# Recurrence of an RWKV layer: substitution steps at other points, the second head's copies on ScalarE

## The chip, the cores and the metric

One core of one Trainium2 chip runs the whole program. The metric is the device time of one execution in microseconds (us); three runs of the kernel before took 3350.44, 3358.05 and 3355.8 us, so their median is 3355.8 us.

## The reference

The reference is two blocks, one after the other. The first has an RWKV-7 mixer beside a pooling branch, a layer norm and a mixture of experts; the second is two attention layers (grouped queries, then latent attention). The change touches only the mixer's recurrence over 1024 tokens and 12 heads of size 64, cut here to its core:

```python
def rwkv7_step(state, inp):
    r, decay, k, v, kk, a = inp
    sa = jnp.einsum('bhij,bhj->bhi', state, -kk)
    state = (state * decay[:, :, None, :]
             + sa[..., None] * (kk * a)[:, :, None, :]
             + v[..., None] * k[:, :, None, :])
    out = jnp.einsum('bhij,bhj->bhi', state, r)
    return state, out
...
    _, y = lax.scan(rwkv7_step, state0, (tmaj(r), tmaj(decay), tmaj(k), tmaj(v), tmaj(kk), tmaj(a)))
```

What the kernel must give is `y`, for all tokens and heads. It does not step token by token: it takes chunks of 64 tokens, and inside a chunk the steps become a triangular system of 64 equations, whose inverse is worked out ahead.

## The kernel before, in words

**Units and slots.** `phase_units` does the mixer's projections and its recurrence. A unit is one pair of heads over 512 tokens, that is 8 chunks; there are 12 units (6 pairs, two halves of the sequence). The work of a unit is cut into lanes: `project` (the three projections, 72 groups of TensorE products with tile `pz`), `tokens`, `within`, `hand_over`, `solve`, `masks`, `inverse`, `chain`, `finish` and a few single calls. Each lane is a generator, and `PLAN` gives for each of its pieces a point, counted from the start of the unit's chain. Units follow each other every 24 points (`SLOT`). The loop at the end of `phase_units` goes through the points in order, and at each point through the lanes in the order of `ORDER` (within, lt_load, chain, finish, inverse, tokens, hand_over, masks, start_state, solve, project, thload). The order of the instructions on every engine, and of the DMAs on SP's queue, is the order in which this loop writes them; the points have no time of their own.

**The chain.** `chain` of a unit takes 24 points, three for each chunk. At the first, TensorE makes `ry` (L784; tiles `cA` for the first head, `cB` for the second) and both halves are copied from PSUM to `R`; at the second, TensorE multiplies `R` by the inverse (`T64`, L789) and both halves are copied to `XA` and `XB`; at the third, TensorE makes the addition to the state (L796) and VectorE writes the next state into `XA` and `XB` (L798). All four copies of a chunk go through `copy` and are VectorE instructions of line L775. Points -24 to -1 of a unit are the 24 steps of the chain of the unit ahead, so that point -17 is step 7 of that chain, -11 its step 13 and -8 its step 16, and point -25 is the last step of the chain before that.

**The inverse.** The 64x64 system is inverted from its 16x16 diagonal blocks. `within` makes the system (`M`) and stores it to DRAM (`labd`, L656); `lt_load` fetches the diagonal blocks into tile `LT` with four DMAs (L664). `solve` does the substitution in 15 steps on VectorE, each a product (L711) and a sum (L713) over t x t elements for step t; each step needs the one before. Its end stores the result to DRAM (`tnd`, L715) and fetches it back into block form with eight DMAs (L720, tile `T16`; the profile writes `T`). `inverse` begins with two transposes of `T16` on VectorE (L737) and a product with it on TensorE (L742, `pA<-T,L`), and ends in `T64`, which the first L789 of the unit's chain needs.

**Queues.** SP issues nearly all DMAs of the phase, in the written order, and stays at one that waits. TensorE, VectorE and ScalarE also run in the written order. `finish` stores its result with SP at its points 37 and 39, which are steps 13 and 15 of the next chain.

Of the kernel before, what the change touches and what calls it, by code (L numbers as in the profile page):

```python
# [142 lines left out]
def phase_lowrank(g, xh0, xl0):  # L143

    nc, tc, a = g.nc, g.tc, g.a
    with ExitStack() as c:
# [231 lines left out]
        -54, -53, -51, -49],  # L378
    "thload": [-57],
    "hand_over": [-21, -18, -18, -18, -17],  # L380
    "solve": [-22, -22, -22, -22, -22, -20, -20, -20, -20, -20, -20, -19, -18, -18, -17, -17],
    "masks": [-21, -20, -19, -16, -16],
    "inverse": [-8, -7, -4, -3, -2, -2, 0, 0, 0],
    "start_state": [-12],
    "within": [-35, -35, -35, -34, -33, -33, -32, -30],
    "tokens": [-47, -47, -46, -45, -44, -44, -43, -42, -41, -41, -40, -39, -38, -37, -37, -36, -34, -33, -33, -31,
        -31, -31, -29],
    "lt_load": [-24],
    "chain": [0, 1, 2, 3, 4, 5, 6, 7, 8, 9, 10, 11, 12, 13, 14, 15, 16, 17, 18, 19, 20, 21, 22, 23],
    "finish": [26, 27, 29, 30, 31, 32, 32, 32, 35, 37, 38, 39, 40, 41, 42],  # L390
}
# [13 lines left out]
def phase_units(g, xh, xl):  # L405
    nc, tc, a = g.nc, g.tc, g.a
    with ExitStack() as c:
# [12 lines left out]
        lo, hi = slice(0, 64), slice(64, 128)  # L420
# [345 lines left out]
        def chain(v):  # L766

            u, q = U[v], v % NPAIR
            u.Y = hv.tile([P, HC, 64], F32, name="Y")
            u.st = hv.tile([P, HC, 6], F32, name="st")  # L770
            hd = ((lo, u.GA, u.XA, u.TK[0], "cA"), (hi, u.GB, u.XB, u.TK[1], "cB"))

            def copy(sl, out, src):
                if True:
                    nc.vector.tensor_copy(out, src)  # L775
                else:
                    nc.scalar.activation(out, src, AF.Copy)

            for cc in range(HC):
                yy = pC.tile([P, 64], F32, name="yy")  # L780
                R = hv.tile([P, 64], F32, name="R")
                for sl, G, X, TK, tag in hd:
                    ry = pC.tile([P, 64], F32, name=tag)
                    nc.tensor.matmul(ry[sl], G[:, cc, 0, :], X[:, 0, cc, :])  # L784
                    copy(sl, R[sl], ry[sl])
                yield
                for e, (sl, G, X, TK, tag) in enumerate(hd):
                    us = pC.tile([P, 64], F32, name=tag)
                    nc.tensor.matmul(us[sl], T64[:, cc, e, :], R)  # L789
                    copy(sl, X[sl, 1, cc, :], us[sl])  # L790
                for sl, G, X, TK, tag in hd:
                    nc.tensor.matmul(yy[sl], G[:, cc, 1, :], X[:, 0, cc, :], start=True, stop=False)
                yield
                for sl, G, X, TK, tag in hd:
                    sp = pC.tile([P, 64], F32, name=tag)
                    nc.tensor.matmul(sp[sl], TK[:, cc, :], X[:, 1, cc, :])  # L796
                    dst = X[sl, 0, cc + 1, :] if cc + 1 < HC else Sc[sl, q, :]
                    nc.vector.scalar_tensor_tensor(dst, X[sl, 0, cc, :], f[sl, v, cc:cc + 1], sp[sl], op0=OP.mult, op1=OP.add)  # L798
                for e, (sl, G, X, TK, tag) in enumerate(hd):
                    nc.tensor.matmul(yy[sl], u.H[:, cc, e, :], X[:, 1, cc, :], start=False, stop=True)  # L800
                nc.scalar.activation(u.Y[:, cc, :], yy, AF.Copy)
                if cc:
                    nc.vector.bn_stats(u.st[:, cc - 1, :], u.Y[:, cc - 1, :])
                yield
            nc.vector.bn_stats(u.st[:, HC - 1, :], u.Y[:, HC - 1, :])
# [2341 lines left out]
```

## Time and profile before

| | us |
|---|---|
| median of three runs | 3355.8 |
| profiled execution, its own time | 3354.52 |
| its span | 3352.7 |
| TensorE busy in the span | 2974.5 (89%) |
| VectorE busy | 2149.2 (64%) |
| ScalarE busy | 1537.0 (46%) |
| GpSimd busy | 1623.5 (48%) |

The recurrence's first chain matmul starts at 265.6 us of the span and its last chunk's at 860.6 us. In the stretch from 265 to 863 us TensorE is busy for 520.99 of 598.00 us, VectorE for 451.70, GpSimd for 363.71 and ScalarE for 244.95. A matmul's end is modelled, and matmuls overlap, so a busy TensorE is not one at its peak. A gap in brackets behind an instruction is idle time of its engine before it, with what ended it.

### The profile page before, as it was taken

What the parts mean: (1) busy time and instruction counts of PE and PEld (TensorE: products, weight loads), DVE (VectorE), ACT (ScalarE), POOL (GpSimd) and SP (SyncE); (2) the same over time, 40 slices, a digit from 0 to 9 for tenths busy, and PEclk for the clock granted to TensorE, in tenths of its full rate; (3) what the DMA queues carried; (4) which work ended last, traced back from release to release, by engine and by line L of the source; (5) the groups of instructions that cost most, each with busy time, mean ns of one, the idle gap of its engine ahead of it and who ended that gap; (6) DMA issues with size and microseconds to landing.
All of it is one profiled execution on the core that took longest, in us unless ns stands there. A gap on an engine that the chain in (4) does not pass through costs nothing. (4 is left out here: it accounts for less than half of the span.)

```text
span 3352.7 us, 47462 instructions
## 1 busy us (share of the span) xinstructions
PE 2974.5 (89%) x16804; PEld 2080.9 (62%) x16804; DVE 2149.2 (64%) x3471; ACT 1537.0 (46%) x2828; POOL 1623.5 (48%) x1564
## 2 busy tenths in 40 slices
PE   7878888888869997799988988989898889999998
PEld 4356656655657765699854554557677755555557
DVE  2147787786469977866346676767347247676666
ACT  3334344343439967533134444545345334444452
POOL 0065666665435543553134545567446215454465
PEclk9888999988869999799999999999999999999999
DMA  8835555445769998423221111246134311111136
GB/s 292 282 106 124 143 123 128 110 121 152 236 230 334 324 327 299 163 89 99 74 70 38 50 39 51 68 139 220 51 97 147 120 50 62 46 42 42 41 102 222
DMA packets 394066, 457.16 MB, mean 136 GB/s; under 512 B 123319, under 2 KB 301970, under 8 KB 393698
## 3 DMA queue, kind: packets, MB, share of 16 engines
q1 hardware_dynamic: 380032, 426.15, 40.7%
q0 software_dynamic: 7616, 17.09, 1.5%
q10 hardware_dynamic: 6178, 10.86, 0.8%
q8 instruction: 133, 2.18, 0.3%
q14 instruction: 107, 0.88, 0.1%
HBM read 329.40 MB, written 101.11 MB: 128 GB/s over the span
## 5 line engine op out<-in xcount | busy, mean ns | idle before, releaser
L2117 ACT ACTIVATE p<-st 128x512 f32<-128x512 f32 (+1 forms) x672 | 378.1, 584 | 391.9 <-PE st L2115 318.5
L2036 DVE TENSOR_REDUCE mx<-s 128x1 f32<-128x1280 f32 x256 | 380.4, 1486 | 260.8 <-PE s L2035 260.8
L2127 POOL TENSOR_TENSOR acc<-acc,p 128x512 f32<-128x512 f32 x256 | 379.3, 1482 | 128.0 <-ACT p L2117 114.7
L2135 PE MATMUL o<-p,V 128*64 128x512 f32 (+1 forms) x1344 | 318.3, 595 | 0.0
L2127 DVE TENSOR_TENSOR acc<-acc,p 128x512 f32<-128x512 f32 x256 | 285.6, 1116 | 7.6
L1419 DVE TENSOR_TENSOR wl<-wr,wh 128x1024 fp32r<-128x1024 f32 x156 | 227.4, 1487 | 40.3 <-ACT wh L1418 40.2
L103 PE MATMUL pz<-xh,wh 128*128 128x512 f32 x440 | 223.8, 509 | 7.7 <-ACT wh L453 7.6
L1418 ACT ACTIVATE wh<-wr 128x1024 fp32r<-128x1024 f32 x192 | 199.0, 1055 | 38.2 <-DMA wr<-in_exp_up_dram 21.2
L105 PE MATMUL pz<-xh,wl 128*128 128x512 f32 x440 | 184.6, 420 | 15.9 <-POOL wl L460 10.2
L104 PE MATMUL pz<-xl,wh 128*128 128x512 f32 x440 | 183.7, 417 | 0.0
L103 PE MATMUL pj<-hh,wh 128*128 128x512 f32 (+1 forms) x416 | 160.5, 386 | 9.2 <-DVE xk L2787 4.5
L2135 PEld LDWEIGHTS o<-p,V 128*64 128x64 f32 x1344 | 81.7, 136 | 139.7 <-issue 135.9
L2127 POOL TENSOR_TENSOR acc<-p 128x512 f32<-128x512 f32 (+1 forms) x40 | 48.6, 1215 | 241.9 <-ACT p L2117 237.5
L1799 POOL TENSOR_TENSOR wl<-wr,wh 128x512 fp32r<-128x512 f32 (+1 forms) x70 | 88.2, 1273 | 151.2 <-ACT wh L1797 150.9
L1419 POOL TENSOR_TENSOR wl<-wr,wh 128x1024 fp32r<-128x1024 f32 x36 | 88.5, 2461 | 148.7 <-ACT wh L1418 133.8
L105 PE MATMUL pj<-hh,wl 128*128 128x512 f32 (+1 forms) x416 | 156.2, 376 | 0.4 <-POOL wl L1799 0.4
L2149 POOL TENSOR_TENSOR rg<-rg,gt 128x512 f32<-128x512 f32 (+1 forms) x40 | 48.6, 1214 | 222.1 <-ACT rg L2148 221.9
L104 PE MATMUL pj<-hl,wh 128*128 128x512 f32 (+1 forms) x416 | 155.9, 375 | 0.0
L2115 PE MATMUL st<-QQ,K 128*128 128x512 f32 (+1 forms) x352 | 150.7, 429 | 2.8 <-ACT p L2117 2.8
L105 PE MATMUL pj<-wh,hl 128*128 128x256 f32 x480 | 141.4, 295 | 4.4 <-POOL hl L1880 4.2
L104 PE MATMUL pj<-wl,hh 128*128 128x256 f32 x480 | 140.6, 293 | 4.7 <-DVE wl L1799 4.7
L103 PE MATMUL pj<-wh,hh 128*128 128x256 f32 x480 | 141.4, 295 | 0.7 <-DVE hh L1879 0.7
(517 smaller groups left out, 8397.6 us busy)
## 6 DMA issues: line engine op xcount, KB each, us to landing
wr<-in_exp_gate_dram SPq DMA_DIRECT2D x64, 512.0 KB
wr<-in_exp_up_dram SPq DMA_DIRECT2D x64, 512.0 KB
wr<-in_exp_down_dram SPq DMA_DIRECT2D x32, 1024.0 KB
w<-in_l_w_out_dram SPq DMA_DIRECT2D x56, 512.0 KB
wm<-in_l_w_mod_dram SPq DMA_DIRECT2D x48, 512.0 KB
w<-in_w_in_dram SPq DMA_DIRECT2D x40, 512.0 KB
wr<-in_l_w_in_dram SPq DMA_DIRECT2D x33, 512.0 KB
y<-ysd SPq DMA_DIRECT2D x16, 512.0 KB
```

The lines of the kernel that those rows point to most:

```text
L103: nc.tensor.matmul(out, lh, rh, start=start, stop=False)
L104: nc.tensor.matmul(out, lh, rl, start=False, stop=False)
L105: nc.tensor.matmul(out, ll, rh, start=False, stop=stop)
L1418: nc.scalar.activation(wh, w, AF.Copy)
L1419: eng.tensor_tensor(wl, w, wh.bitcast(F32), op=OP.subtract)
L1799: eng.tensor_tensor(st["l"][:, ks], st["w"][:, ks], st["h"][:, ks].bitcast(F32), op=OP.subtract)
L2036: nc.vector.tensor_reduce(m[:, j:j + 1], ps.rearrange("p a b -> p (a b)")[:, :SK], axis=AX.X, op=OP.max)
L2115: nc.tensor.matmul(st[:, :n], kk[:, kt * P:(kt + 1) * P], qv[:, pt.q0:pt.q0 + n], start=(j == 0), stop=(j == len(passes) - 1))
L2117: nc.scalar.activation(p[:, :n], st[:, :n], AF.Exp, scale=self.scale)
L2127: eng.tensor_tensor(a, r.p[r.kts[0], e][:, :n] if r.first else a, r.p[r.kts[i], e][:, :n], op=OP.add)
L2135: nc.tensor.matmul(pt.po[64 * e:64 * e + 64, :n], pt.out["V"](e, kt), r.p[kt, e][:, :n], start=(r.first and i == 0), stop=(r.last and i == ...
L2149: nc.gpsimd.tensor_tensor(rg[:, :n], rg[:, :n], pt.gt[:, :n], op=OP.mult)
```

## The change

Three things change. The pieces of `solve` go to other points: before, points -22 (5 steps), -20 (6), -19, -18 and -17; after, one step at most points from -25 to -12, two at -21, and steps 14 and 15 with the store and the eight fetches at -11. `lt_load` goes from point -24 to -27. And `copy` in `chain` gives the second head's copies to ScalarE.

```diff
-    "solve": [-22, -22, -22, -22, -22, -20, -20, -20, -20, -20, -20, -19, -18, -18, -17, -17],
+    "solve": [-25, -24, -23, -22, -21, -21, -20, -19, -18, -16, -15, -13, -12, -11, -11, -11],
...
-    "lt_load": [-24],
+    "lt_load": [-27],
...
             def copy(sl, out, src):
-                if True:
+
+                if sl == lo:
                     nc.vector.tensor_copy(out, src)
                 else:
                     nc.scalar.activation(out, src, AF.Copy)
```

`inverse` keeps its points (-8, -7, -4, -3, -2, -2, 0, 0, 0), and TensorE's order of instructions is as before.

## Rows read from the trace of the kernel before

**Rows 1.** The page: busy time, share of the span and instructions of each engine.
```profile
PE 2974.5 (89%) x16804; PEld 2080.9 (62%) x16804; DVE 2149.2 (64%) x3471; ACT 1537.0 (46%) x2828; POOL 1623.5 (48%) x1564
```
**Rows 2.** Busy time by stretch, one chain each (third and seventh unit); header first.
```profile
core 0: us, PE busy (x) PEld busy (x) DVE busy (x) ACT busy (x) POOL busy (x), PEclk, DMA share, GB/s
...
365.16:414.03 48.87, 43.03 (x425) 29.96 (x425) 38.88 (x110) 21.45 (x40) 33.04 (x47) 0.97 0.61 167
...
566.21:616.62 50.41, 45.17 (x425) 31.36 (x424) 39.99 (x110) 21.50 (x40) 31.90 (x47) 0.90 0.47 116
```
**Rows 3.** TensorE's waits, 265 to 863 us: us in total, times, longest us.
```profile
PE cA L784 <- DVE XA L798: 43.6, 32, 5.5
PE cA L789 <- DVE R L775: 17.2, 20, 2.5
PE cA L796 <- DVE XA L775: 4.7, 10, 1.4
```
**Rows 4.** VectorE in order of time, steps 6 to 15 of one solve (start, duration).
```profile
476.00 0.44 DVE L711 TENSOR_TENSOR pr<-Tn,LT 64x36 f32<-64x36 f32 x1
...
480.22 0.27 DVE L713 TENSOR_REDUCE Tn<-pr 64x11 f32<-64x121 f32 x1
...
484.67 0.53 DVE L711 TENSOR_TENSOR pr<-Tn,LT 64x196 f32<-64x196 f32 x1
485.23 0.35 DVE L713 TENSOR_REDUCE Tn<-pr 64x14 f32<-64x196 f32 x1
...
487.64 1.05 DVE L711 TENSOR_TENSOR pr<-Tn,LT 64x225 f32<-64x225 f32 x1
488.73 0.38 DVE L713 TENSOR_REDUCE Tn<-pr 64x15 f32<-64x225 f32 x1
```
**Rows 5.** TensorE in order of time in the same chain, two of its gaps.
```profile
480.84 0.33 PE L784 MATMUL cA<-XA,GA 128*64 128x64 f32 x2 [1.03 <-DVE XA L798]
...
489.47 0.48 PE L784 MATMUL cA<-XA,GA 128*64 128x64 f32 x2 [1.99 <-DVE XA L798]
```
**Rows 6.** TensorE in order of time, steps 16 to 18 of that chain.
```profile
505.19 0.64 PE L742 MATMUL pA<-T,L 128*64 128x64 f32 x16
...
507.59 0.33 PE L784 MATMUL cA<-XA,GA 128*64 128x64 f32 x2 [0.87 <-DVE XA L798]
```
**Rows 7.** Groups by line, 265 to 863 us: count, busy us, mean ns, idle before.
```profile
L711 DVE TENSOR_TENSOR pr<-Tn,LT 64x1 f32<-64x1 f32 (+4 forms) x165 | 79.3, 481 | 5.0 <-DMA LT<-labd 0.5
...
L713 DVE TENSOR_REDUCE Tn<-pr 64x1 f32<-64x1 f32 (+4 forms) x165 | 38.1, 231 | 5.7
```
**Rows 8.** Groups by line, 265 to 863 us: copies, and ScalarE's copy of Y.
```profile
L801 ACT ACTIVATE Y<-yy 128x64 f32<-128x64 f32 x95 | 21.2, 223 | 208.3 <-PE yy L800 206.2 <-POOL mv L823 1.8
...
L775 DVE COPY R<-cB 64x64 f32<-64x64 f32 x96 | 21.8, 227 | 3.0
```
**Rows 9.** ScalarE in order of time, step 5 of the same chain.
```profile
477.84 1.28 ACT L833 ACT_TABLE_LOAD   x1
```
**Rows 10.** VectorE in order of time, steps 13 and 23 of that chain.
```profile
499.49 0.69 DVE L649 TENSOR_TENSOR M<-pA,const 128x512 f32<-128x512 f32 x1 [0.27 <-PE pA L644]
500.09 0.20 DVE L775 COPY XA<-cA 64x64 f32<-64x64 f32 x1
...
515.88 0.23 DVE L805 BATCH_NORM_STATS2 st<-Y 128x6 f32<-128x64 f32 x1 [0.54 <-ACT Y L801]
```
**Rows 11.** SP's queue in order of time, same chain: issue and its duration.
```profile
489.13 0.50 SPq L715 DMA_DIRECT2D tnd<-Tn  x1
491.11 3.92 SPq L720 DMA_DIRECT2D T<-tnd  x8
...
512.20 1.80 SPq L664 DMA_DIRECT2D LT<-labd  x4
```
**Rows 12.** SP, VectorE and TensorE in order of time before the first chain.
```profile
229.05 1.82 SPq L664 DMA_DIRECT2D LT<-labd  x4
...
232.38 0.15 DVE L711 TENSOR_TENSOR pr<-Tn,LT 64x1 f32<-64x1 f32 x1 [0.92 <-DMA LT<-labd]
...
246.35 0.38 DVE L713 TENSOR_REDUCE Tn<-pr 64x15 f32<-64x225 f32 x1
...
258.93 1.15 PE L742 MATMUL pA<-T,L 128*64 128x64 f32 x32
```

## The prediction

> **What bounds the kernel now.** I read the page's totals first: TensorE is busy for 89% of the span, VectorE for 64% [rows 1], so TensorE sets the time unless it is made to wait. The stretch of the change, about 600 of the 3353 us, is then read by chain. A chain takes some 50 us, and TensorE is idle for 48.87 - 43.03 = 5.84 us of one and 50.41 - 45.17 = 5.24 us of another [rows 2]. The two also show what the clock does: the same 425 matmuls take 2.14 us more at a granted clock of 0.90 than at 0.97, so a hundredth of the clock is worth 0.31 us. Third, who ends those idle times: nearly all are VectorE's, 43.6 us for the state of L798, 17.2 us for `R` and 4.7 us for `XA` [rows 3], 65.5 us together. VectorE is busy for 39 to 40 us of a chain [rows 2], and where its solve steps stand in a heap, the chain's small instructions queue behind them. Rows 4 show one heap: six steps from 476.00 to 480.49, behind which L798 comes late and TensorE stands for 1.03 us [rows 5]; step 15 (487.64 to 489.11), behind other VectorE work, is followed by a gap of 1.99 us.
>
> **What the spreading returns.** In the chain of rows 5 the gaps behind solve heaps lie at steps 4, 6, 7, 8 and 9. Not every gap of rows 3 is the solve's: one per unit, 0.87 us at step 18, follows the two transposes L737 [rows 6] and stays. So 65.5 - 10 x 0.87 = 56.8 us, over 11 chains that carry a solve 5.2 us each, are behind heaps. A step of the solve costs 0.48 + 0.23 = 0.71 us on average [rows 7]; one per point mostly fits between the chain's instructions, and I take 0.4 us per chain as what is still waited for. That is 4.8 us returned.
>
> **The second head's copies.** Sixteen VectorE copies per chain, 0.23 us each [rows 8], go to ScalarE, so 3.7 us of VectorE time per chain. ScalarE's copy of Y from PSUM takes 0.22 us for twice the partitions [rows 8], and I take that for the moved ones. The best case would be all 3.7 us, if every copy were on the path; but TensorE needs both halves, so a step gets shorter by one copy only where VectorE is late, and those steps are counted already. I add 0.2 us per chain, for the step in which T64 is written behind `R`. What hides the moved copies is ScalarE's own idle time: it is idle for 208.3 us before its Y copies, waiting for TensorE [rows 8], and busy for 21 us of a chain [rows 2]. Behind a moved copy stand, in ScalarE's order, the squares and exponentials of `tokens` and the weight splits; their users are several points away. In front can stand a table load of 1.28 us [rows 9], with the logarithms at step 5 and another load at step 6; TensorE has transposes and projection products there. Without that cover the worst case is both loads on the path, 2.6 us per chain; I take 0, as that idle time is ten times as long.
>
> **The new wait.** The solve now ends at point -11 and not -17, while `inverse` still starts at -8. Count from the copy to `XA` at step 13. Now it ends at 500.29, and TensorE reaches the first product with T16 at 505.19 [rows 10, 6]: 4.9 us. After the change, steps 12 and 13 stand ahead of that copy: 2 x 0.8 us, less one copy of 0.23 us that left and the 0.27 us that VectorE idles at 499.49 [rows 10], so it comes 1.1 us late. Behind it stand steps 14 and 15: 0.53 + 0.35 + 1.05 + 0.38 = 2.31 us [rows 4]. Then the way through DRAM, which is the same as before: the solve ends at 489.11, the store is issued at 489.13, the eight fetches at 491.11, and their issue ends at 495.03 [rows 4, 11]. No row shows when the last lands, since nobody waits for it; for `LT`, issue ended at 230.87 and VectorE could start at 232.38 [rows 12], 1.5 us later. From below I put 1.0 us, from above 2.0 us; I take 1.2, as only one small fetch is left at the end. That is 2.00 + 3.92 + 1.2 = 7.1 us. Together 1.1 + 2.3 + 7.1 = 10.5 us against 4.9: T16 comes 5.6 us after TensorE wants it. TensorE stands at L742 and VectorE at L737, both in order, so the chain behind them stands too, and nothing hides it. Part comes back: while they wait the copies of step 16 get done, so that from T16 on only the two transposes and L798 are left before step 18, about 1.8 us in place of 507.59 - 505.19 = 2.4. The wait costs 5.6 - 0.6 = 5.0 us per chain.
>
> A row and a rule differ here on the price of a step. Step 15 took 1.05 us, step 14 only 0.53 us for 13% fewer elements [rows 4]. The Trainium skill, page "SBUF — State Buffer", section "SBUF: two separate sides", says that VectorE with two SBUF inputs and GpSimd lock a shared port pair for a whole instruction, and that the loser is blocked. By that rule every step which starts behind a GpSimd instruction pays step 15's price, which speaks against spreading them; by the row's mean of 0.48 us most do not. It is the first rival.
>
> **LT and SP's queue.** Between points -27 and -24 SP has no other DMA of a usual unit, and LT's fetch waits for the store of `labd` ahead of it, so moving it changes nothing: 0. But step 1 now comes at the end of the chain, at 516.1 (after L805, [rows 10]); the fetch's issue ended at 514.0 [rows 11], so with 1.5 us it lands at 515.5: just in time, and a late one would cost its lateness, 0 to 1 us per unit. After the change the SP queue holds the eight fetches longer, but the chain is as much later. I take 0. The stores of `finish` at step 15 come behind the fetches; their reader is far away.
>
> **Ends of the phase.** The first solve lies before any chain. VectorE's steps ran from 232.38 to 246.73, and L742 came at 258.93 [rows 12], 12.2 us after the end, with the DRAM way of 7.1 us hidden. Ended at -11, with three points to go to `inverse`, the solve ends somewhere between 247 and 258.9, so T16 comes 4.8 us before to 7.1 us after its use; I take an end at 256, since it now stands behind `within`'s masks: +4 us, once. In the chain from 365 to 414 us the tokens of the second half are loaded, which shows in a DMA share of 0.61 against 0.47 [rows 2]; the fetches share the DMA engines with them, between 0 and 4 us, and I take 1.5. The last two chains with a solve have less VectorE work beside it, so perhaps smaller heaps and the same wait: between -1 and +3 each, I take +1.
>
> **The clock.** Chains at 0.90 against 0.97 differ by 2.1 us. Without the gaps at steps 4 to 9 the drops there should be rarer, while the new wait makes one; I take 0.4 us returned in each of nine chains, -3.6.
>
> **The sum.** Eleven chains: -(4.8 + 0.2) + 5.0 = 0 each, together 0. Ends +4 + 1.5 + 2, clock -3.6: +4 us, of 3354.5 us (the span of 3352.7 and 1.8 around it): 3358. The median is 1.3 us above the profiled time. The heaps' gaps have turned into one wait.
>
> **Rivals.** (1) *Later rows, slower.* If the spread steps pay what step 15 pays, steps 12 to 15 cost up to 0.5 us more each (1.05 against 0.53, [rows 4]); the solve then ends 2 us later, and every microsecond goes straight into the wait for T16 at step 16. It decides as soon as the solve ends over 2.5 us after the copy of step 13. 11 x 2 = 22: 3380. For it: 1.05 us; against: the mean of 0.48 us [rows 7].
> (2) *Shorter wait, faster.* With a VectorE relieved of 3.7 us, steps 12 and 13 fit into its idle time (-1.1) and step 15 takes what step 14 takes (-0.5); the heaps return all 5.2 us and the clock 0.6 more (two hundredths). About -2.5 us per chain, 10 chains: 3358 - 25 = 3333. For it: VectorE is idle in a fifth of each chain [rows 2]; against: T16's way of 7.1 us stays longer than the 4.9 us it has.
> (3) *The clock.* A TensorE that stands for 4 us at a stretch may run behind it at 1.2 GHz; at 0.90 in place of 0.97 in eight of the chains, 8 x 2.1 = 17: 3375. For it, a chain at 0.90 is already found [rows 2]; against, the drops now follow gaps of 2 us and would go. The Trainium skill, page "TensorE: Matmul & The Clock Gate", Part 1, has the clock fall when the engine idles and come back with activity; by that rule every wait of this length brings it about, which is the 3375.
>
> **How the numbers follow.** The forecast, even trade: 0.40, with 3347 to 3368 for itself. Rival 1: 0.25; rival 2: 0.25; rival 3: 0.10. A difference of 0.2% (6.7 us) is about what can be told from none. The forecast gives 0.27 to same, 0.08 to slower, 0.05 to faster; rival 2 gives 0.23 to faster and 0.02 to same; rival 1 is slower, rival 3 slower with 0.09 and same with 0.01. That is faster 0.28, same 0.30, slower 0.42. The range takes in rivals 1 and 2 nearly whole: 3332 to 3384.
>
> **What would show it.** TensorE's waits should lose most of the 65.5 us and have a new row: L742 (`pA<-T,L`), waiting for the DMA of T, some 4 us in each of ten chains, with VectorE's L737 beside it. L775's `cB` groups should be ScalarE's, at about 0.22 us. If L742 does not wait for T, the forecast is wrong on the fast side; if L784 and L789 still wait for VectorE in steps 3 to 9 as before, on the slow side.

## The result: slower by 1.1%, and the profile after

The changed kernel takes 3387.25 us (median of five runs, 3377.09 to 3396.04); five runs of the kernel before, on the same chip, have a median of 3350.44 us. The ratio is 1.0107, 95% interval 1.0086 to 1.0128. The forecast was 3358, its range 3332 to 3384; it had 4 us for the change, and the medians differ by 36.8 us. The profiled execution took 3385.53 us, its span is 3383.8, so 31.1 us more than the span of before. 5.9 us of that lie ahead of the first chain (its first matmul comes at 271.5 and not at 265.6 us), 21.0 us in the twelve chains, and 4.2 us behind them, where nothing was changed.

Two profiled executions also differ where the programs are the same, and the 5.9 us hide that. Nothing that was moved stands ahead of the first unit's store of `labd` (L656), and yet it is issued at 225.62 us before and at 221.14 us after. From there to the first chain it is 39.94 us before and 50.32 us after, so this lead-in has become longer by 10.4 us (windows, columns as in [rows 2], before and after):

```profile
225.62:265.56 39.94, 32.09 (x238) 24.34 (x236) 26.00 (x52) 16.54 (x25) 28.63 (x38) 0.91 0.59 138
```

```profile
221.14:271.46 50.32, 36.73 (x235) 26.71 (x233) 26.25 (x52) 16.84 (x25) 30.09 (x38) 0.80 0.48 111
```

In the rows of after, every line number from 774 on is one higher than in those of before (L784 is L785, L789 is L790, L796 is L797, L798 is L799); the kept copies are L776 and the moved ones L778. First the page's totals, to be read against [rows 1]:

```profile
PE 2981.2 (88%) x16804; PEld 2076.6 (61%) x16804; DVE 2086.7 (62%) x3279; ACT 1584.5 (47%) x3020; POOL 1650.7 (49%) x1564
```

VectorE has 192 instructions and 62.5 us less, ScalarE 192 instructions and 47.5 us more. TensorE's waits from 240 to 905 us (us in total, times, longest us) stand against [rows 3]:

```profile
PE pA L742 <- DMA T<-tnd: 34.2, 10, 5.2
PE cA L797 <- DVE XA L776: 15.9, 10, 3.4
PE cB L797 <- ACT XB L778: 10.8, 11, 1.1
PE cA L790 <- DVE R L776: 8.5, 18, 0.7
PE pA L644 <- DVE BK L611: 8.4, 19, 0.7
PE cA L785 <- DVE XA L799: 7.6, 9, 3.6
PE pA L742 <- DMA mix<-yf: 6.4, 2, 4.3
```

The wait for the state fell from 43.6 to 7.6 us and that for `R` from 17.2 to 8.5. The wait for T16 at L742 is new. The longest of its ten, 5.2 us, lies in the lead-in; in the chains the list puts nine of L742's waits down to T16 and two, 6.4 us, to another DMA of SP's queue (`mix`), so that L742 is waited for in all eleven chains that carry a solve. Three more have come or grown: L797 for VectorE's `XA` (4.7 us before), L797 for ScalarE's `XB`, and L644 for `BK` (0.5 before). Next, VectorE in order of time in the fifth chain, at the solve's steps 12 to 15 (start, duration; 64x144 is step 12, 64x225 step 15):

```profile
505.48 2.31 DVE L611 TENSOR_TENSOR BK<-th,EN 64x512 f32<-64x512 f32 x2
507.81 0.82 DVE L711 TENSOR_TENSOR pr<-Tn,LT 64x144 f32<-64x144 f32 x1
508.67 0.29 DVE L713 TENSOR_REDUCE Tn<-pr 64x12 f32<-64x144 f32 x1
...
509.79 0.96 DVE L711 TENSOR_TENSOR pr<-Tn,LT 64x169 f32<-64x169 f32 x1
510.79 0.32 DVE L713 TENSOR_REDUCE Tn<-pr 64x13 f32<-64x169 f32 x1
511.03 0.67 DVE L649 TENSOR_TENSOR M<-pA,const 128x512 f32<-128x512 f32 x1
511.63 0.21 DVE L776 COPY XA<-cA 64x64 f32<-64x64 f32 x1
511.76 0.48 DVE L711 TENSOR_TENSOR pr<-Tn,LT 64x196 f32<-64x196 f32 x1
512.28 0.35 DVE L713 TENSOR_REDUCE Tn<-pr 64x14 f32<-64x196 f32 x1
512.66 0.54 DVE L711 TENSOR_TENSOR pr<-Tn,LT 64x225 f32<-64x225 f32 x1
513.23 0.38 DVE L713 TENSOR_REDUCE Tn<-pr 64x15 f32<-64x225 f32 x1
```

No bracket stands behind any instruction from 499 to 515 us: VectorE does not idle once. The spread steps stand between L611, L649 and others, large instructions of `tokens` and `within`, and the chain's small copies wait behind both. TensorE in order of time shows what that costs, at steps 8, 12, 14 and 16 of the chain (the bracket is its idle time before the row; L644 is a piece of `within`, and its gap is counted at step 12, as it follows that step's products):

```profile
498.39 0.27 PE L797 MATMUL cB<-XB,TK 128*64 128x64 f32 x1 [1.05 <-ACT XB L778]
507.93 1.13 PE L644 MATMUL pA<-G,BK 64*128 64x128 f32 x14 [0.68 <-DVE BK L611]
511.89 0.27 PE L797 MATMUL cA<-XA,TK 128*64 128x64 f32 x1 [1.38 <-DVE XA L776]
520.50 1.12 PE L742 MATMUL pA<-T,L 128*64 128x64 f32 x16 [3.87 <-DMA T<-tnd]
```

For the first of them ScalarE in order of time gives the reason. The product that the moved copy reads (L790) is done at 495.7; the copy starts at 498.12, 2.4 us later, behind a table load and four others, for which the prediction took 0:

```profile
494.41 1.28 ACT L836 ACT_TABLE_LOAD   x1
495.71 0.21 ACT L836 ACTIVATE mv<-mv 128x8 f32<-128x8 f32 x1
495.82 0.71 ACT L586 ACTIVATE sq<-sq,const 128x512 f32<-128x512 f32 x1
496.55 0.60 ACT L691 ACTIVATE TK<-pA 128x512 f32<-128x512 f32 x1
497.05 1.05 ACT L453 ACTIVATE wh<-w 128x1024 fp32r<-128x1024 f32 x1
498.12 0.22 ACT L778 ACTIVATE XB<-cB 64x64 f32<-64x64 f32 x1
```

For the last, SP's queue and VectorE's second transpose of T16 (against [rows 11, 6]):

```profile
513.64 0.49 SPq L715 DMA_DIRECT2D tnd<-Tn  x1
515.60 3.65 SPq L720 DMA_DIRECT2D T<-tnd  x8
```

```profile
520.44 0.71 DVE L737 STREAM_TRANSPOSE T16T<-T 64x512 f32<-64x512 f32 x1 [1.07 <-DMA T<-tnd]
```

The solve ends at 513.61 and the transpose starts at 520.44: 6.8 us through DRAM.

### The profile page after: what moved, and what is told of

It is laid out like the page before. It is cut to its first block, busy times and chain, and to the rows that moved or that the text cites. A ratio compares the mean times of both kernels' runs of the same rounds, so it can differ in the third digit from the quotient of the medians.

```text
span 3383.8 us, 47607 instructions
## 1 busy us (share of the span) xinstructions
PE 2981.2 (88%) x16804; PEld 2076.6 (61%) x16804; DVE 2086.7 (62%) x3279; ACT 1584.5 (47%) x3020; POOL 1650.7 (49%) x1564
## 5 line engine op out<-in xcount | busy, mean ns | idle before, releaser
L460 POOL TENSOR_TENSOR wl<-w,wh 128x256 fp32r<-128x256 f32 x144 | 111.7, 807 | 65.0 <-ACT wh L453 65.0
```

The lines of the kernel that those rows point to most:

```text
L460: nc.gpsimd.tensor_tensor(wl[:, c0:c0 + 2], w[:, c0:c0 + 2], wh[:, c0:c0 + 2].bitcast(F32), op=OP.subtract)
```

## The experiments

Each ratio is against the kernel before, run beside it on the same chip; where two experiments of different groups are compared, it is by their ratios. Going in, theory A said that the points make the loss and the copies are neutral, theory B that the copies on ScalarE eat what the spreading returns.

**The points alone.** `solve` and `lt_load` as in the change, `copy` as before.

> The new points of solve and lt_load alone; all copies stay on VectorE. Theory A (the points make the loss: T16 comes late at step 16, and the steps left at 8 to 13 hold up the chain; the copies are neutral): about as long as the whole change, 3377 to 3395 us, with L742 waiting 30 to 40 us for T16. Theory B (ScalarE's copies come late, some 1.1 us per chain at step 8 and 0.5 at others, and so eat what the spreading returned): 3355 to 3372 us, and no wait for XB at step 8.

Measured: 3406.27 us, ratio 1.0167 (1.0143 to 1.0191). Longer than the whole change, and above both ranges; B is out, and A is right on the points and wrong on the copies.

**The copies alone.** `copy` as in the change, `solve` and `lt_load` as before.

> The second head's copies on ScalarE alone, with the old points. Theory A: between 3340 and 3358 us, since TensorE waits for VectorE's half anyway. Theory B: ScalarE's table load, exponential and wh split ahead of a moved copy show at step 8 here too, 10 to 16 us over the phase: 3360 to 3372 us, with a row L796 waiting for ScalarE's XB.

Measured: 3321.04 us, ratio 0.9916 (0.9894 to 0.9938). Neither theory held: the copies alone are a gain of 27 us. The two parts together, 1.0167 x 0.9916 = 1.0082, come near the whole (1.0107).

**Early points**, alone and with the copies.

```diff
-    "solve": [-22, -22, -22, -22, -22, -20, -20, -20, -20, -20, -20, -19, -18, -18, -17, -17],
+    "solve": [-25, -24, -24, -23, -23, -22, -22, -21, -21, -20, -20, -19, -19, -18, -17, -17],
-    "lt_load": [-24],
+    "lt_load": [-27],
```

> The steps spread from point -25 to -18, two at most points, so that the solve ends at -17 as before and T16 is there in time; copies on VectorE. Theory A: no wait at L742, and 2.8 to 4.8 us per chain come back: 3300 to 3325 us. Rival C (VectorE owes the chain the same time wherever the steps stand; two steps per point, 1.4 us, still hold up a step of the chain): 3340 to 3358 us, with TensorE's waits for R, XA and the state near 65 us in sum.

> As the early points, with the second head's copies on ScalarE as well. Theory A: within 5 us of the early points alone, or up to 8 us less, since VectorE is relieved of 3.7 us per chain beside the steps. Theory B: 10 to 16 us more than the early points alone, at steps 7 and 8, with L796 waiting for ScalarE's XB.

Measured: 3334.81 us, 0.9962 (0.9944 to 0.9979), and 3325.95 us, 0.9930 (0.9909 to 0.9951). No wait for T16 in either, so spreading is not bad by itself; but alone it returned 13 us, less than A's 25 to 50, and TensorE's gaps at step 9 rose (20.1 us over all chains before, 25.3 now). With the copies it is no better than the copies alone: `XB` at step 8 costs 10.7 us, and the gaps at step 1 are 18.0 us, where the copies alone have 4.9. There, as below with T16 unread, the solve's first step waits for `LT` (15.8 us, nine times) with `T64`'s last piece behind it.

Now the theory was: the loss is the wait for T16, and a step costs where VectorE is already full. The next four runs tested both, and a third place for the steps.

**Steps at 1 to 6**, with the copies and `lt_load` as in the change:

```diff
+    "solve": [-23, -23, -23, -22, -22, -22, -21, -21, -21, -20, -20, -19, -19, -18, -18, -18],
```

> The second head's copies on ScalarE; the solve at points -23 to -18 (three steps each at chain steps 1 to 3, two each at 4 to 6, where VectorE's other work leaves most room), so it ends one point before the old one. If a step costs only where VectorE is already full: the gaps at steps 4 to 9, 42 us with the copies alone, fall below 20 us: 3298 to 3312 us. Rival (VectorE owes the time wherever it stands; the gaps turn up at steps 2 to 5): 3317 to 3328 us, like the copies alone (3321) and the early points with copies (3326).

Measured: 3315.40 us, 0.9904 (0.9883 to 0.9925). Between the two expectations: TensorE's gaps at steps 4 to 9 fell from 42.0 (copies alone) to 23.6 us, those at 10 to 12 rose from 6.8 to 19.2.

**The change with T16 unread.** `inverse` reads another tile of the same size, so the kernel leaves out what the solve worked out.

```diff
-                nc.vector.transpose(T16T[sl, :, e, :], T16[sl])
+                nc.vector.transpose(T16T[sl, :, e, :], L32[sl, :, 0, :])
...
-            yield from mul(ps, L16, T16)
+            yield from mul(ps, L16, L32[:, :, 0, :])
...
-            nc.vector.tensor_tensor(T32, ps, T16, op=OP.add)
+            nc.vector.tensor_tensor(T32, ps, L32[:, :, 0, :], op=OP.add)
```

> The whole change, but the inverse reads L32 in the place of T16 (other values, the same sizes), so that nobody waits for the eight fetches. If the way through DRAM is what costs, as I priced it (5.0 us per chain): 3387 - 55 = 3332 us. If the wait is worth its 35 us of idle time and a slower clock behind it: 3335 to 3345 us, and the gaps at steps 10 to 15 stay near 34 us. Rival (another wait takes its place at steps 16 to 18): over 3365 us.

Measured: 3379.38 us, 1.0091 (1.0074 to 1.0108). The wait for T16 is gone and almost nothing came back (5 us by the ratios, with intervals that overlap): another wait took its place, though not where I had put it. TensorE's waits of this run, and VectorE and TensorE in order of time from step 23 of the fifth chain to step 1 of the sixth:

```profile
PE cA L790 <- DVE T L763: 30.9, 10, 5.6
```

```profile
527.78 0.15 DVE L711 TENSOR_TENSOR pr<-Tn,LT 64x1 f32<-64x1 f32 x1 [1.91 <-DMA LT<-labd]
...
529.11 1.40 DVE L763 TENSOR_TENSOR T<-pA,T32T 64x512 f32<-64x512 f32 x2
```

```profile
529.92 0.30 PE L790 MATMUL cA<-R,T 128*64 128x64 f32 x2 [1.78 <-DVE T L763]
```

The first step of the next solve, at point -25, waits for `LT`, and `T64`'s last piece (L763) is queued behind it on VectorE. In the whole change the chain's stand at step 16 gave `LT` its time: from the issue of `labd`'s store to the next chain's first product it is 8.0 to 10.4 us there, and 4.9 to 6.5 us here (first nine chains). The two waits lie behind each other, and taking one away uncovers the other.

**The change with small late steps.** Steps 9 to 15 work on one element and leave out the others.

```diff
             for t in range(1, 16):
+                w = t if t < 9 else 1
-                nc.vector.tensor_tensor(pr[:, :t, :t], Tn[:, 0:t, 0:t]...
+                nc.vector.tensor_tensor(pr[:, :w, :w], Tn[:, 0:w, 0:w]...
...
```

> The whole change, but steps 9 to 15 of the solve work on one element each (wrong values; the points, the order, the store and the eight fetches stay), so VectorE has some 4 us less to do per chain, nearly all of it at chain steps 6 to 13. If VectorE's fullness at steps 8 to 13 makes both the gaps there and T16's lateness: the gaps at 10 to 15 fall from 34 us to under 10, the wait at L742 from 35 to 5 to 15 us, 3310 to 3335 us. If the DRAM way alone makes it: L742 still waits for 25 us or more, 3355 to 3375 us.

Measured: 3356.30 us, 1.0020 (1.0008 to 1.0033). The time is the second expectation's, though L742 waits for 22.8 us and not for 25. The gaps at steps 10 to 15 fell from 33.8 to 25.1 us only, since the first matmuls of `within` (L644) come late there too. What the run took away is worth 29 us (1.0107 - 1.0020); the DRAM way stays.

A step of one element is not always a short one. Two of them in the fifth chain, and the GpSimd instructions that run beside the second:

```profile
479.24 0.14 DVE L712 TENSOR_TENSOR pr<-Tn,LT 64x1 f32<-64x1 f32 x1
...
491.80 0.57 DVE L712 TENSOR_TENSOR pr<-Tn,LT 64x1 f32<-64x1 f32 x1
```

```profile
488.67 3.69 POOL L610 TENSOR_TENSOR BK<-kn,EN 64x256 f32<-64x256 f32 x4
```

Beside the first no GpSimd instruction runs. The second starts inside the last of the four L610, which ends at 492.36, and ends at 492.37. Steps 10 to 13 so take 0.57 to 0.69 us in that chain, one element or not; this run therefore prices the elements of the late steps, and not the late steps.

**One copy back.** As the steps at 1 to 6, with the third chunk's X copy on VectorE.

```diff
-                    copy(sl, X[sl, 1, cc, :], us[sl])
+                    copy(lo if cc == 2 else sl, X[sl, 1, cc, :], us[sl])
```

> As the solve at steps 1 to 6 with copies on ScalarE, but the X copy of the third chunk (chain step 7, where a table load, an exponential, TK and a weight split stand ahead of it on ScalarE) goes back to VectorE. If ScalarE's XB sets the 1.1 us gap at step 8: 8 to 14 us less than with all copies on ScalarE. Rival (VectorE's XA is as late): within 4 us of it.

Measured: 3310.64 us, 0.9882 (0.9863 to 0.9901), the fastest version here, 1.2% below the kernel before and 2.2% below the changed one. Against the same points with all copies on ScalarE it is 4.8 us, with intervals that overlap: not told apart. `XB` no longer waits (3.2 us there), but the gap at step 9 rose from 4.9 to 11.1 us.

The last four were to separate T16, `LT` and the gaps at 10 to 15.

**T16 unread, later start**; and **the change with the later start**, which reads T16. Both have

```diff
-    "solve": [-25, -24, -23, -22, -21, -21, -20, -19, -18, -16, -15, -13, -12, -11, -11, -11],
+    "solve": [-23, -23, -23, -22, -21, -21, -20, -19, -18, -16, -15, -13, -12, -11, -11, -11],
```

> T16 unread as before (the inverse reads L32), and the first three steps of the solve at point -23 in place of -25, -24 and -23, so that they no longer stand ahead of T64's last step while LT is still on its way. If the 31 us at step 1 of the run with T16 unread were LT's wait, and it ate what the wait for T16 had cost: both are gone, 40 us less idle time and a faster clock, 3325 to 3345 us, and what is left above the copies alone (3321) is the gaps at steps 10 to 15. Rival (the gaps at 10 to 15 and their clock carry the loss): 3360 us or more.

> The whole change with its first three steps at point -23 (T16 read again). If LT is late only when T16 is not (the chain's stand at step 16 gives LT its time): within 8 us of the whole change, 3379 to 3395 us, L742 waiting 30 to 36 us for T16. Rival (the early start itself costs, in steps 0 to 2): 3365 to 3378 us.

Measured: 3336.89 us, 0.9957 (0.9942 to 0.9972), and 3374.96 us, 1.0070 (1.0047 to 1.0093). With both waits gone the changed points are within 0.4% of the copies alone: the T16 wait and the `LT` wait behind it are worth 50 us (1.0107 - 0.9957), the rest of the spreading 14 (0.9957 - 0.9916). Reading T16 again costs 38 us. The later start by itself brings the changed kernel some 12 us, in its rival's range, but the intervals still touch (1.0086 to 1.0093), and the rival's reason is not shown: the gaps at steps 0 to 3 are 5.4 us in place of 7.0; TensorE idles as long in the chains as with the whole change (103.7 against 100.4 us); and of the 5.8 us by which its first chain starts earlier 3.5 lie ahead of the first store of `labd`, where the two kernels are the same.

**Only the R copies**, with the old points, and **steps at 1 to 5**, with one copy back and `lt_load` as in the change:

```diff
-                    copy(sl, X[sl, 1, cc, :], us[sl])
+                    copy(lo, X[sl, 1, cc, :], us[sl])
```

```diff
+    "solve": [-23, -23, -23, -23, -22, -22, -22, -21, -21, -20, -20, -20, -19, -19, -19, -19],
```

> Old points; only the second head's R copies go to ScalarE, its X copies stay on VectorE. If what pays is that the two heads' copies run beside each other wherever VectorE is late (gaps at steps 4 and 7 belong to R): about half of the 27 us of all copies, 3331 to 3340 us. If it is VectorE's relieved time as such: also half. If ScalarE's XB copies at step 8 are a burden: 3315 to 3325 us, less than or like all copies (3321).

> As the solve at steps 1 to 6 with one copy back on VectorE (3310.6), but packed into steps 1 to 5 (4, 3, 2, 3 and 3 steps). If the gaps at steps 7 to 9 (26 us) come from the solve's last steps at step 6 that push VectorE's later work back: 10 to 15 us less, 3296 to 3302 us. Rival (steps 7 to 9 are full with the tokens' own VectorE work, and three large steps at step 5 make a new gap at step 6): 3308 to 3318 us.

Measured: 3343.93 us, 0.9977 (0.9961 to 0.9992), and 3322.04 us, 0.9907 (0.9887 to 0.9926). The R copies bring 8 us and the X copies the larger part, which none of the three expectations had. Whether the copies pay because VectorE has less to do or because the two heads' copies run beside each other, no run here separates. Packing the steps closer is worse: the gap at step 7 grows to 23.3 us, behind three large steps at step 5.

## Where the time went, by stretches and steps

The windows of the twelve chains, from their first L784 to their last matmul (columns as in [rows 2]; the first is the length, the second TensorE's busy time, the one behind POOL the granted clock), in turn the kernel before, after, the points alone and the copies alone:

```profile
265.56:864.12 598.56, 521.55 (x4896) 358.14 (x4895) 452.00 (x1260) 244.41 (x444) 363.71 (x524) 0.91 0.49 128
```

```profile
271.46:891.00 619.54, 519.01 (x4896) 358.65 (x4895) 392.89 (x1068) 291.71 (x636) 380.36 (x522) 0.91 0.48 124
```

```profile
269.31:921.47 652.16, 538.34 (x4896) 370.48 (x4895) 461.80 (x1260) 241.23 (x444) 375.01 (x524) 0.88 0.46 118
```

```profile
260.07:828.30 568.23, 503.58 (x4896) 345.73 (x4895) 402.67 (x1068) 290.36 (x636) 373.17 (x522) 0.96 0.52 135
```

Length less busy time is what TensorE idles. The table splits it by the step of the chain at which the gap stands (gaps of 0.05 us and more in order of time, each with the last step whose chain products have begun, summed over the chains; us):

| steps | before | points alone | copies alone | after | T16 unread | and later start | fastest |
|---|---|---|---|---|---|---|---|
| 0 to 3 | 7.8 | 12.2 | 4.9 | 7.0 | 34.4 | 4.6 | 4.3 |
| 4 to 9 | 54.6 | 13.1 | 42.0 | 24.2 | 24.4 | 30.3 | 28.4 |
| 10 to 12 | 0.9 | 31.4 | 6.8 | 14.4 | 13.6 | 16.4 | 14.3 |
| 13 to 15 | 4.2 | 21.8 | 3.8 | 19.4 | 15.7 | 16.3 | 3.4 |
| 16 | 0 | 34.9 | 0 | 35.4 | 0 | 0 | 0 |
| 17 to 23 | 9.3 | 0 | 6.6 | 0 | 9.1 | 8.6 | 6.8 |
| all | 76.8 | 113.4 | 64.1 | 100.4 | 97.2 | 76.2 | 57.2 |

The reader is to see three things. The points alone empty steps 4 to 9 (41.5 us returned) and fill 10 to 16 with more than that. In the row of steps 4 to 9 the eleventh chain has 11.4 us before and 11.8 after, and 8.8 to 13.0 in every run here, wherever the solve's steps stand; the gaps behind the heaps are the rest. And the length moves by more than the idle time: between before and the copies alone TensorE idles 12.4 us less (length less busy time), but its same 4896 matmuls are also busy for 18.0 us less, with the granted clock at 0.96 in place of 0.91.

## Why the prediction was wrong

**The step that failed: "one per point mostly fits between the chain's instructions, and I take 0.4 us per chain as what is still waited for."** Of the 5.2 us per chain that I put behind the heaps, 4.8 were to come back. The first part of the error is the 5.2 itself: the eleventh chain's 11.4 us at steps 4 to 9 are no heap's, since they stay in every run. The ten other chains have 43.1 us there before, 4.3 each, and 12.0 after, of which 10.6 are the copies' gap at step 8; so the heaps' gaps did go. The second part is the 0.4: steps 10 to 12, where only 0.9 us stood, have 14.4 after the change, 1.4 us for each of the ten chains. I had measured the heaps that the steps leave and not the places to which they go. The trace of before shows those places, in rows that the prediction does not have. VectorE, in order of time, at steps 10 to 12 of the chain of [rows 5]:

```profile
492.29 0.22 DVE L775 COPY XA<-cA 64x64 f32<-64x64 f32 x1 [0.47 <-PE cB L789]
...
494.81 0.75 DVE L518 SCALAR_TENSOR_TENSOR z<-pz,pcol,z 128x511 f32<-128x511 f32 x1 [0.95 <-ACT z L517]
...
496.54 1.38 DVE L611 TENSOR_TENSOR BK<-th,EN 64x512 f32<-64x512 f32 x2
```

From 489.1 to 500.3 us VectorE idles for 0.47, 0.95 and, ahead of L649 [rows 10], 0.27 us only. Four large steps of 1.1 to 1.3 us each (10 to 13, product and sum) were moved into these 1.7 us and the 0.9 us that four moved copies leave. "VectorE is idle in a fifth of each chain" [rows 2] is true, but of the 10.4 us of one chain only 1.7 lie here.

The steps also got dearer by the move, and the price of 0.71 us for one did not hold there. The products of steps 11 and 15, in the chains before and then after (count, busy us, mean ns):

```profile
L711 DVE TENSOR_TENSOR pr<-Tn,LT 64x121 f32<-64x121 f32 x11 | 4.3, 393 | 0.4
L711 DVE TENSOR_TENSOR pr<-Tn,LT 64x225 f32<-64x225 f32 x11 | 11.1, 1010 | 0.0
```

```profile
L711 DVE TENSOR_TENSOR pr<-Tn,LT 64x121 f32<-64x121 f32 x11 | 9.4, 856 | 0.0
L711 DVE TENSOR_TENSOR pr<-Tn,LT 64x225 f32<-64x225 f32 x11 | 6.0, 548 | 0.4
```

The products of steps 10 to 13 took 22.0 us in all before and 36.5 after, 1.3 us more per chain, just where VectorE is full; steps 3, 4, 9 and 15 became cheaper by about as much (26.8 to 12.9). The price goes with whether a GpSimd instruction runs when the step starts. Step 12's product took 0.38 to 0.40 us in the nine solves of before where none does, and 0.81 to 0.82 us in nine of after where one has 0.55 us left; of the changed kernel's 165 products in the chains 113 start beside one, and each of them ends only after it. No run takes GpSimd's work away from these steps, so how much of the 14.4 us it makes stays open.

**The wait for T16** came as forecast, at the place and for the reason given, and a little smaller. From the copy of step 13 (ends at 511.84) to L742 it is 8.7 us; for that stretch I had 9.4 (2.3 + 7.1). Steps 14 and 15 took 1.75 us and not 2.31, and the way through DRAM is 6.8 us against 7.1. Steps 13 to 18 together cost 19.4 + 35.4 - 13.5 = 41.3 us more, 3.8 per chain, where I had 5.0. The two runs with the later start show it by experiment: reading T16 or not is 3374.96 against 3336.89, 38 us where I had 55 (11 x 5.0), and without that wait the kernel is no longer slower than before.

**The copies** I priced at 0.2 us of gain and at 0 on ScalarE. Both are off, in opposite directions. ScalarE's `XB` at step 8 costs 10.8 us in all, 1.0 per chain, because 3.7 us of its other work (from the table load at 494.41 on) run up to it; its idle share of one half said nothing about that stretch. But the part alone is a gain of 27 us, and beside the new points it is worth 20 us (1.0167 against 1.0107). I had argued that a step gets shorter by one copy only where VectorE is late and that those steps were counted; they were counted as returned by the spreading, which they were not.

**`LT`**: I wrote that a late one would cost 0 to 1 us per unit and took 0. It did cost little in the changed kernel (3.6 us, three times), but only because T16 was later. Uncovered, it was 34.4 - 4.6 = 29.8 us in the phase, 2.7 per chain.

**The ends and the clock.** From the store of `labd` to the first chain the lead-in cost 10.4 us; I had 4. L742 waits there for 5.2 us, and TensorE's work takes 36.73 us at a granted clock of 0.80 where it took 32.09 at 0.91. The clock was to return 3.6 us; TensorE's busy time in the chains fell by 2.5 us, so for the chains of the whole change that term was about right, by a balance of old drops and new ones. For the parts it was not: the points alone add 16.8 us of busy time at a clock of 0.88, the copies alone take away 18.0. My slope of 0.31 us per hundredth and chain gives 12 x 5 x 0.31 = 18.6 us for 0.91 to 0.96, which fits, and 11.2 us for 0.91 to 0.88, which is too little.

**The rivals.** Rival 1 has the time nearest to the outcome (3380), but that is luck: of its mechanism one half came. Steps 12 and 13 did get dearer, and 10 and 11 with them; 14 and 15 did not, so in the fifth chain the solve ends 1.8 us behind the copy of step 13 and not over 2.5, and what the dearer steps cost falls on steps 10 to 14 and not on the wait for T16. Against this rival I had set the mean of 0.48 us; it was no evidence, since the heaps' steps paid already. The 16 elements of step 4 took 509 ns in the heap and 176 ns spread. By the Trainium skill, page "SBUF — State Buffer", section "SBUF: two separate sides", a VectorE instruction with two inputs in SBUF and a GpSimd instruction that reads SBUF exclude each other, and the later of the two is blocked until the first has ended. The trace agrees, product by product, as with the one-element steps of 0.14 and 0.57 us; in sum nothing shows, 80.0 us for all L711 against 79.3. Rival 3's time did not come, as the granted clock is 0.91 in the chains before and after. Its mechanism did: in nine of the eleven chains the clock falls to 0.50 with the wait at L742, and in the other two it is there already; but drops behind the old gaps went.

Of what the prediction said would show it, L742's wait came, and the moved copies took 0.22 us. But the waits of 65.5 us, which were to lose most of their time, lost half: 32.0 us are left (7.6 for the state, 8.5 for `R`, 15.9 for `XA`), and `XA`'s has grown from 4.7. None of the marks looked at the steps to which the work had gone.

## What to carry to other kernels

Before a piece of work is moved on an engine, read that engine's rows where it will land, as closely as those where it now stands; a busy share over the whole stage hides a part that is full, and a neighbour's instructions there can double the price of the piece, as GpSimd's did here. When a wait is to be taken away, ask which wait ends just before it: here two of them, T16 and `LT`, covered each other, and removing T16's alone brought 5 us, or none, where both brought 50. And parts of one change can have opposite signs: alone, the copies were a gain of 0.8% and the points a loss of 1.7%.

## What was not expected of the hardware

A small instruction of VectorE can stand behind one of GpSimd without a wait in the profile. In the run with small late steps 110 of the 165 products in the chains start while a GpSimd instruction runs; all of them end after it, half of them at most 14 ns after it, and the profile counts that time as VectorE's busy time.

TensorE's clock follows the gaps to another place. In the fifth chain before, the granted clock falls to 0.50 (1.2 GHz) at 489.0 us, with the gap behind step 15 of the solve; after, it falls at 520.4 us, when TensorE goes on after 3.87 us without work at L742, and stays high in the 40 us ahead, in spite of the gaps of 0.6 to 1.4 us there. That is one chain, and no rule for short gaps: in the fourth and seventh of the changed kernel it falls at 462.4 and 616.0 us already, with the gap of 1.38 us at step 14. The windows of both, before and after:

```profile
489.00:495.80 6.80, 6.33 (x29) 4.27 (x29) 5.03 (x14) 1.50 (x2) 4.16 (x6) 0.50 0.15 21
```

```profile
520.40:523.80 3.40, 3.30 (x46) 3.11 (x47) 1.72 (x5) 1.04 (x3) 0.00 (x0) 0.50 0.82 226
480.00:520.00 40.00, 31.68 (x262) 21.49 (x258) 30.01 (x78) 22.03 (x45) 33.22 (x46) 1.00 0.40 102
```

So a gap can cost more than its own length: of the copies' 30.3 us in the chains, 12.4 are idle time and 18.0 are matmuls that ran faster. No run holds the clock and changes the gaps alone, so the split rests on the rows of one execution each and not on an experiment of its own.
